# First norm's sum of squares from the token layout on ScalarE, early low parts on VectorE, and a fourth early feature tile

## The chip, the cores and the metric

The kernel runs on one core of one Trainium2 chip. The metric is the device time of one execution in microseconds (us). Three runs of the kernel before took 835.93, 838.29 and 835.86 us; the median is 835.93. A core has five engines, each with a queue of its own that it works through strictly in order: TensorE (PE in the trace; its weight loads are PEld), VectorE (DVE), ScalarE (ACT), GpSimdE (POOL) and SyncE (SP), which here only issues DMAs. Engines wait for each other through semaphores. SBUF is the on-chip working memory, and PSUM, which takes TensorE's results, has eight banks of 128 x 512 float32.

## The reference, cut to what matters

One decoder layer on 512 tokens of width 1024, all in float32. Only its beginning matters here:

```python
h = rms_norm(x, norm_mix_w)          # x * rsqrt(mean(x*x over the 1024 features) + 1e-6) * w
proj = h @ w_in                      # 1024 -> 5664 columns
z, xbc, dt_raw, q, k, v, f_raw = split(proj)
y_ssd = ssd_mixer(xbc, z, dt_raw)    # conv over 4 tokens, silu, chunked scan (4 chunks, 16 heads), gated norm
y_fox = fox_mixer(q, k, v, f_raw)    # attention with forgetting, 16 heads
x = x + concat(y_ssd, y_fox) @ w_out
x = x + conv_gated_mlp(rms_norm(x))  # 1024 -> 5632 -> 2816 -> 1024
```

## The kernel before, in words

Each float32 product is made of three multiplies on rounded halves: an operand is cast to a high part (ScalarE), and the low part is the operand less the high part (VectorE or GpSimdE). `mm3` (lines 108 to 112) issues high x high, low x high and high x low. `load_split` (lines 99 to 106) brings a 128 x 1024 weight tile in by SyncE (`wraw`, five buffers), casts it on ScalarE (`wh`, L104) and takes its low part (`wl`, L105). `wh` and `wl` have two buffers each, so a third weight tile can only be cast when TensorE has finished with the first.

The input comes twice: as `xT` (features on partitions, eight pieces `xr`), from which the operands `xh` (L181, ScalarE) and `xl` (L182, VectorE) are made, and as `x` (tokens on partitions, tile `x2`), which is the residual. The rms factor of the first norm is not applied to the input but to the results: `R` holds the factor of each token spread over 128 partitions, and `r` and `rhalf` hold it with tokens on partitions.

The work around the change, in the order of the program:

- Lines 192 to 214: eight warm-up multiplies into `spin`; then for each of the eight pieces the operands, the squares of the piece (L204 on ScalarE for pieces 1, 3, 5, 7, L206 on GpSimdE for the others), and on TensorE the dt/f projection `pdt` (L211, L212) and the first feature tile `b0` (weight `wxbc[8]`), 40 multiplies in all.
- Lines 232 to 239: the weight `second` (`wxbc[10]`), seven additions of the squares on VectorE (L234), four multiplies with a column of ones that sum over partitions into `spin` (L237), and `token_scale` (lines 136 to 144): mean and epsilon (L121), power -1/2 (L122, GpSimdE), a diagonal matrix (`diag`, L139), a multiply with ones that spreads it (`rbc`, L143), and the copy into `R` (L144, ScalarE).
- Line 597: three feature tiles are multiplied ahead of their turn (`early`): 8, 10 and 0. `feature_tile` (lines 222 to 230) issues 24 multiplies of 512 columns.
- `dt_f` (lines 262 to 316): a chain of small VectorE operations on `pdt` to the cumulative sums `cs` (L304, L307), which go out to DRAM (`cs_d`) and come back spread over partitions as `sc` (L395).
- `ssd_proj(g)` (lines 335 to 377): for six feature tiles the evacuation with `R` (`xp`, L344, VectorE), the convolution (L347 on ScalarE, three L351 on VectorE), tanh (L355) and its product (L356), and transposes (L360); then the two halves of `z` in `token_block` (four weight tiles), evacuated by L374 to L376.
- `ssd_scan(g)` (lines 385 to 450), four chunks: masked exponentials (L404, L409), their product with C B (L412), `yd` (L415), `yo` and the state.

Which engine takes a low part is told by the table `LOW_PART` (lines 36 to 51): the n-th call with a key takes the n-th letter, `d` for VectorE, `p` for GpSimdE; a key that isn't there means GpSimdE (`second`, and the four tiles of the first `z`). A scheduler orders the instructions of each engine by its own simulated timeline, with the code under `high_priority` first. So a change at the beginning also reorders rows that it doesn't touch. PSUM: three banks in pool `pg` (`pdt`, `b0` and `spin` to begin with), four in `pm` (`mbank`), one in `po`.

Of the kernel before, what the change touches and what calls it, by code (L numbers as in the profile page):

```python
# [8 lines left out]
F32 = mybir.dt.float32  # L9
F32R = mybir.dt.float32r  # L10
AF = mybir.ActivationFunctionType
ALU = mybir.AluOpType
# [3 lines left out]
P = 128  # L16
SEQ = 512
D = 1024
NK = D // P
NTB = SEQ // P  # L20
# [11 lines left out]

AHEAD = 2000
WARM = 8
ACT_SQ = (1, 3, 5, 7)
LOW_PART = {
    "feat": "pddddddddp",
    "o0": "dp",
# [17 lines left out]
def tile_hybrid_layer(  # L56
# [19 lines left out]
    nc = tc.nc  # L76
    act, dve, pool, pe = nc.scalar, nc.vector, nc.gpsimd, nc.tensor
# [5 lines left out]
    po = ctx.enter_context(tc.tile_pool(name="po", bufs=1, space=PSUM))  # L83
# [4 lines left out]
    def raw(ap):  # L88
        return ap.bitcast(F32)
# [3 lines left out]
    def low_part(key):  # L93
        order = LOW_PART.get(key, "p")
        n = taken.get(key, 0)
        taken[key] = n + 1
        return dve if order[n % len(order)] == "d" else pool

    def load_split(src, sub=None):
        r = wp.tile([P, 1024], F32, tag="wraw", name="wraw", bufs=5)  # L100
        nc.sync.dma_start(r, src)
        h = wp.tile([P, 1024], F32R, tag="wh", name="wh")
        l = wp.tile([P, 1024], F32R, tag="wl", name="wl")
        act.copy(h, r)  # L104
        (sub or dve).tensor_tensor(out=l, in0=r, in1=raw(h), op=ALU.subtract)  # L105
        return h, l

    def mm3(o, ah, al, bh, bl, start, stop, grouped=True):
        kw = {} if grouped else {"skip_group_check": True}
        pe.matmul(o, ah, bh, start=start, stop=False, **kw)  # L110
        pe.matmul(o, ah, bl, start=False, stop=False, **kw)  # L111
        pe.matmul(o, al, bh, start=False, stop=stop, **kw)  # L112

    def bank(name="g"):
        return pg.tile([P, 512], F32, tag="g", name=name)

    def mbank(name="m"):
        return pm.tile([P, 512], F32, tag="m", name=name)

    def rsqrt(dst, src, scale, shape):  # L120
        dve.tensor_scalar(out=dst, in0=src, scalar1=scale, scalar2=EPS, op0=ALU.mult, op1=ALU.add)  # L121
        pool.tensor_tensor(out=dst, in0=dst, in1=mhalf[:, 0 : shape], op=ALU.pow)  # L122
# [4 lines left out]
    ones = cp.tile([P, P], F32, tag="ones", name="ones")  # L127
# [6 lines left out]
    x2 = cp.tile([P, NTB, D], F32, tag="x2", name="x2")  # L134

    def token_scale(rr, bc, ss, diag_pool):
        rsqrt(rr, ss, 1.0 / D, NTB)
        dg = diag_pool.tile([P, NTB, P], F32, tag="diag", name="diag", bufs=1)
        dve.tensor_mul(  # L139
            dg, ident[:, None, :].broadcast_to([P, NTB, P]), rr[:, :, None].broadcast_to([P, NTB, P])  # L140
        )
        ps = mbank("rbc")
        pe.matmul(ps, ones, dg.rearrange("p a b -> p (a b)"), start=True, stop=True)  # L143
        act.copy(bc, ps)  # L144
# [6 lines left out]
    R = pa.tile([P, SEQ], F32, tag="R", name="R")  # L151
    r = cp.tile([P, NTB], F32, tag="r", name="r")
# [7 lines left out]
    px = px_ctx.enter_context(tc.tile_pool(name="px", bufs=1))  # L160
# [3 lines left out]
    def load_x(k):  # L164
        xr = px.tile([P, SEQ], F32, tag="xr", name="xr", bufs=NK)
        nc.sync.dma_start(xr, xT[k])
        return xr

    def load_first(half):
        c = slice(half * 512, (half + 1) * 512)  # L170
        w = px.tile([P, 512], F32, tag="wr", name="wr", bufs=2)
        nc.sync.dma_start(w, wxbc[8][:, c])
        return c, w

    def split_first(c, w):
        act.copy(first[0][:, c], w)
        dve.tensor_tensor(out=first[1][:, c], in0=w, in1=raw(first[0][:, c]), op=ALU.subtract)

    def split_x(k, xr):
        w = pc[:, C_MIX + k : C_MIX + k + 1]  # L180
        act.activation(xh[:, k, :], xr, AF.Copy, scale=w)  # L181
        dve.scalar_tensor_tensor(  # L182
            out=xl[:, k, :], in0=xr, scalar=w, in1=raw(xh[:, k, :]), op0=ALU.mult, op1=ALU.subtract
        )

    def load_dt():
        w = px.tile([P, NK, 32], F32, tag="wdr", name="wdr")
        nc.sync.dma_start(w.rearrange("p k m -> p (k m)"), wdtf)
        act.copy(wdt[:, :, 0:32], w)
        pool.tensor_tensor(out=wdt[:, :, 32:64], in0=w, in1=raw(wdt[:, :, 0:32]), op=ALU.subtract)  # L190

    pdt, b0, spin = bank(), bank(), bank()
    for _ in range(WARM):
        pe.matmul(spin[:, :P], ones, ones, start=True, stop=True)
    load_dt()
    sqs = []
    for k in range(NK):
        xr = load_x(k)
        if k == 0:
            nc.sync.dma_start(pc[:, 0:NK], pcol[:, 0:NK])  # L200
        split_x(k, xr)
        sq = px.tile([P, SEQ], F32, tag="sq", name="sq", bufs=NK)
        if k in ACT_SQ:
            act.activation(sq, xr, AF.Square)  # L204
        else:
            pool.tensor_tensor(out=sq, in0=xr, in1=xr, op=ALU.mult)  # L206
        sqs.append(sq)
        if k in (1, 3):
            split_first(*load_first(k // 2))
    for k in range(NK):  # L210
# [11 lines left out]
    def feature_tile(src, o=None):  # L222
        h, l = src if isinstance(src, tuple) else load_split(src, sub=low_part("feat"))
        o = bank() if o is None else o
        for k in range(NK):
            mm3(
                o, h[:, k * P : (k + 1) * P], l[:, k * P : (k + 1) * P], xh[:, k, :], xl[:, k, :],
                k == 0, k == NK - 1,
            )
        return o  # L230

    second = load_split(wxbc[10], sub=low_part("second"))
    for k in range(1, NK):
        dve.tensor_add(sqs[0], sqs[0], sqs[k])  # L234
    with tc.high_priority(AHEAD):
        for tb in range(NTB):
            pe.matmul(spin[:, tb : tb + 1], sqs[0][:, tb * P : (tb + 1) * P], ones[:, 0:1], start=True, stop=True)  # L237
        token_scale(r, R, spin[:, 0:NTB], px)
    dve.tensor_scalar(out=rhalf, in0=r, scalar1=0.5, scalar2=None, op0=ALU.mult)
    px_ctx.close()  # L240

# [352 lines left out]
    def urgent():  # L594
        return tc.high_priority(AHEAD)

    early = {8: b0, 10: feature_tile(second), 0: feature_tile(wxbc[0], po.tile([P, 512], F32, tag="o", name="j0"))}
    dt_f()
    st0 = ssd_proj(0)
    with urgent():  # L600
        m0 = ssd_scan(0, *st0)
    for tb in range(NTB):
        nc.sync.dma_start(x2[:, tb, :], x[tb * P : (tb + 1) * P, :])
    st1 = ssd_proj(1)
    for pair in range(2):
        out_proj((pair,), m0[2 * pair : 2 * pair + 2])
# [135 lines left out]
    def up_proj(fs, cuts):  # L742
        ws = [load_split(wup[f]) for f in fs]
        os = [bank("up") for _ in fs]
        w = SEQ // cuts
        for cut in range(cuts):
            s = slice(cut * w, (cut + 1) * w)
            for o, (h, l) in zip(os, ws):
                for k in range(NK):
                    ks = slice(k * P, (k + 1) * P)  # L750
                    mm3(
                        o[:, s], h[:, ks], l[:, ks], hh[:, k, s], hl[:, k, s], k == 0 and cut == 0, k == NK - 1,
                        grouped=cuts == 1,
                    )
        return os

    early = up_proj((0, NFF), 2)
# [9 lines left out]
    def gated(j):  # L767
        both = []
        for part in range(2):
            f = part * NFF + j  # L770
            o = early[part] if j == 0 else up_proj((f,), 1)[0]
            xp = pu.tile([P, SEQ], F32, tag="up", name="up", bufs=3)
            dve.tensor_mul(xp, o, R2)  # L773
            a = pu.tile([P, SEQ], F32, tag="ua", name="ua", bufs=5)
            cw = C_FCW + 3 * f
            act.activation(a, xp, AF.Identity, scale=pc[:, cw + 2 : cw + 3], bias=pc[:, C_FCB + f : C_FCB + f + 1])  # L776
            for s in range(1, 3):
                dve.scalar_tensor_tensor(  # L778
                    out=a[:, s:], in0=xp[:, : SEQ - s], scalar=pc[:, cw + 2 - s : cw + 3 - s], in1=a[:, s:],
                    op0=ALU.mult, op1=ALU.add,  # L780
                )
            both.append(a)
        act.activation(both[0], both[0], AF.Silu)
        return both
# [12 lines left out]
    for j in range(NH):  # L797
# [5 lines left out]
        k, val = gated(j + NH)  # L803
# [39 lines left out]
    for n, (quarter, _, tiles, start, adds) in enumerate(PRODUCTS):  # L843
# [7 lines left out]
        for u, (lo, hi) in enumerate(UNITS):  # L851
# [14 lines left out]
            for k, i, (lo_, _, h_, l_) in todo:  # L866
# [6 lines left out]
                if k == NH - 1:  # L873
                    for row, col, op, done in adds:
                        tb = row + i
# [85 lines left out]
```

## Time and profile before

| | |
|---|---|
| median of three runs | 835.93 us |
| the profiled execution's own time | 839.82 us |
| its span, first to last instruction | 838.0 us |
| mean granted TensorE clock over the span | 0.995 of full |
| busy: PE, DVE, ACT, POOL | 810.0, 630.9, 435.9, 290.5 us |
| idle TensorE before instructions of the first 140 us, as the trace names it | L212 1.44, L237 0.74, L360 0.75, L306 1.48, L428 0.50, L446 1.73, L415 0.34 us |
| chain that ended last | PE 73%, DVE 11%, issue 6%, POOL 3%, ACT 3%, DMA 2% |

Busy time is a modelled length from an instruction's start to its end; multiplies overlap, so the distance of two starts says more of TensorE's pace than a length. "Idle before" an instruction names what ended the wait of its engine. The times are those of one execution; the profiled one took 3.89 us more than the median of the runs.

### The profile page before, as it was taken

How to read it: one execution, taken by the hardware profiler on the slowest of the kernel's cores; microseconds unless marked ns; L12 is line 12 of the kernel's file. 1: busy time of each engine (PE TensorE's matmuls, PEld its weight loads, DVE VectorE, ACT ScalarE, POOL GpSimd, SP SyncE). 2: the span in 40 equal slices, each digit the busy share in tenths (PEclk: the TensorE clock that was granted, in tenths of full speed). 3: DMA queues.
4: the chain of work that ended last, by engine and by line, in shares of the span. 5: the costliest groups of instructions: out<-in, count | busy, mean ns of one | idle time of the engine just before them, and what ended most of it. 6: DMA issues, size and time to landing. Idle time of an engine off the chain costs nothing.

```text
span 838.0 us, 12428 instructions
## 1 busy us (share of the span) xinstructions
PE 810.0 (97%) x4590; PEld 700.4 (84%) x4590; DVE 630.9 (75%) x1015; ACT 435.9 (52%) x845; POOL 290.5 (35%) x281
## 2 busy tenths in 40 slices
PE   8999989899979999899999999999999999999997
PEld 5788879779979899799898898888888888888885
DVE  7596898775759798898999667666666666887744
ACT  5346645434456687576566255444433444656531
POOL 4125253365535445125233423333333332133120
PEclk9999999999989999999999999999999999999999
DMA  8424332341333333243422244233233223399992
GB/s 315 158 83 131 101 94 85 104 136 51 113 102 106 100 100 112 84 120 101 126 72 66 90 121 134 100 98 101 101 101 99 82 96 101 115 253 182 208 190 84
DMA packets 31565, 98.76 MB, mean 118 GB/s; under 512 B 4048, under 2 KB 5136, under 8 KB 31504
## 3 DMA queue, kind: packets, MB, share of 16 engines
q1 hardware_dynamic: 28048, 86.43, 31.9%
q0 software_dynamic: 3456, 11.54, 7.6%
q8 instruction: 36, 0.59, 0.3%
q14 instruction: 25, 0.20, 0.1%
HBM read 91.56 MB, written 2.20 MB: 112 GB/s over the span
## 4 chain that ended last, share of the span: by engine, by line
PE 73%; DVE 11%; issue 6%; POOL 3%; ACT 3%; DMA 2%; SPq 0%; DVEq 0%; POOLq 0%; ACTq 0%
PE up L112 10%; PE up L111 9%; PE up L110 9%; PE pq L111 4%; PE pq L112 4%; PE pq L110 4%; PE po L112 3%; PE po L111 3%; PE po L110 3%; DVE xs L351 2%; PE Y L110 2%; PE Y L112 2%; PE Y L111 2%; PE o L580 2%; PE pT L566 1%
## 5 line engine op out<-in xcount | busy, mean ns | idle before, releaser
L104 ACT CAST wh<-wraw 128x1024 fp32r<-128x1024 f32 x103 | 108.5, 1053 | 137.6 <-PE up L111 72.1
L110 PE MATMUL pq<-wh,xh 128*128 128x256 f32 x512 | 146.7, 289 | 0.0
L112 PE MATMUL pq<-wh,xl 128*128 128x256 f32 x512 | 146.7, 287 | 0.0
L111 PE MATMUL pq<-wl,xh 128*128 128x256 f32 x512 | 145.6, 285 | 0.5 <-DVE wl L105 0.5
L112 PE MATMUL up<-hh,wl 128*128 128x512 f32 (+1 forms) x368 | 140.2, 381 | 0.2 <-DVE wl L105 0.2
L111 PE MATMUL up<-hl,wh 128*128 128x512 f32 (+1 forms) x368 | 139.9, 380 | 0.0
L110 PE MATMUL up<-hh,wh 128*128 128x512 f32 (+1 forms) x368 | 139.8, 380 | 0.0
L105 POOL TENSOR_TENSOR wl<-wraw,wh 128x1024 fp32r<-128x1024 f32 x31 | 75.1, 2424 | 108.9 <-ACT wh L104 99.9
L105 DVE TENSOR_TENSOR wl<-wraw,wh 128x1024 fp32r<-128x1024 f32 x72 | 89.5, 1243 | 20.0 <-ACT wh L104 19.9
L111 PEld LDWEIGHTS pq<-wl,xh 128*128 128x128 f32 x512 | 98.2, 192 | 1.9 <-DVE wl L105 0.9
L110 PEld LDWEIGHTS pq<-wh,xh 128*128 128x128 f32 x512 | 98.0, 192 | 1.9 <-issue 1.2
L112 PEld LDWEIGHTS pq<-wh,xl 128*128 128x128 f32 x512 | 98.2, 192 | 0.7 <-issue 0.5
L112 PEld LDWEIGHTS up<-hh,wl 128*128 128x128 f32 x368 | 69.2, 188 | 13.5 <-DVE wl L105 0.4
L110 PEld LDWEIGHTS up<-hh,wh 128*128 128x128 f32 x368 | 69.1, 188 | 13.3 <-issue 0.2
L111 PEld LDWEIGHTS up<-hl,wh 128*128 128x128 f32 x368 | 69.2, 188 | 13.2
L773 DVE TENSOR_TENSOR up<-up,R 128x512 f32<-128x512 f32 x44 | 30.3, 691 | 57.0 <-PE up L112 57.0
L778 DVE SCALAR_TENSOR_TENSOR ua<-up,pc,ua 128x511 f32<-128x511 f32 (+1 forms) x88 | 67.2, 766 | 3.2 <-ACT ua L776 1.7
L526 POOL TENSOR_SCALAR bias<-cum,tokS 128x256 f32<-128x256 f32 (+1 forms) x32 | 22.5, 711 | 91.2 <-DVE nm L541 91.2
L545 ACT ACTIVATE prob<-prob,nm 128x128 f32<-128x128 f32 (+1 forms) x64 | 35.9, 562 | 29.6 <-DVE nm L541 29.3
L254 DVE TENSOR_TENSOR x<-po,x 128x512 f32<-128x512 f32 x64 | 43.3, 684 | 10.1 <-PE po L112 9.5
L734 ACT CAST wh<-T 128x1024 fp32r<-128x1024 f32 (+1 forms) x30 | 29.3, 978 | 37.5 <-PE Z L112 15.6
L735 DVE TENSOR_TENSOR wl<-T,wh 128x1024 fp32r<-128x1024 f32 (+1 forms) x30 | 33.8, 1133 | 19.7 <-ACT wh L734 19.7
(237 smaller groups left out, 1862.9 us busy)
## 6 DMA issues: line engine op xcount, KB each, us to landing
wraw<-in_wup_dram SPq DMA_DIRECT2D x44, 512.0 KB, 3.3
wraw<-in_wqkv_dram SPq DMA_DIRECT2D x24, 512.0 KB, 3.3
T<-in_wdown_dram POOLq DMA_DIRECT2D x20, 512.0 KB, 7.8
wraw<-in_wout_dram SPq DMA_DIRECT2D x16, 512.0 KB, 3.3
wraw<-in_wxbc_dram SPq DMA_DIRECT2D x11, 512.0 KB, 4.6
T<-in_wdown_dram SPq DMA_DIRECT2D x10, 512.0 KB, 5.1
wraw<-in_wdown_dram SPq DMA_DIRECT2D x10, 512.0 KB, 3.7
wraw<-in_wz_dram SPq DMA_DIRECT2D x8, 512.0 KB, 3.3
```

The lines of the kernel that those rows point to most:

```text
L104: act.copy(h, r)
L105: (sub or dve).tensor_tensor(out=l, in0=r, in1=raw(h), op=ALU.subtract)
L110: pe.matmul(o, ah, bh, start=start, stop=False, **kw)
L111: pe.matmul(o, ah, bl, start=False, stop=False, **kw)
L112: pe.matmul(o, al, bh, start=False, stop=stop, **kw)
L254: dve.tensor_add(dst, o, dst)
L526: (dve if qb == 2 else pool).tensor_scalar(out=b, in0=cum[:, :n], scalar1=-1.0, scalar2=edge, op0=ALU.mult, op1=ALU.add)
L545: act.activation(p, p, AF.Exp, scale=-1.0, bias=nm[:, qb : qb + 1], accum_out=sm[:, qb : qb + 1])
L734: act.copy(h[:, :n], src[:, :n])
L735: dve.tensor_tensor(out=l[:, :n], in0=src[:, :n], in1=raw(h[:, :n]), op=ALU.subtract)
L773: dve.tensor_mul(xp, o, R2)
L778: dve.scalar_tensor_tensor(out=a[:, s:], in0=xp[:, : SEQ - s], scalar=pc[:, cw + 2 - s : cw + 3 - s], in1=a[:, s:], op0=ALU.mult, op1=ALU.add,
```

## The change

The squares are no longer made from the `xT` pieces and added up. The four loads of `x2` move to the front of the program, ScalarE squares each token block with an accumulated sum per token, and `token_scale` reads that sum. The low parts of `second` and of tile 0's weight are put on VectorE, and tile 0's weight is loaded ahead with `second`. A fourth tile, 1, is multiplied early, into a bank of `pm`. Since tile 0's weight no longer takes a letter of the key `feat`, the letters move on by one tile. In all, the low parts of wxbc[10], wxbc[0] and wxbc[7] go from GpSimdE to VectorE, and that of wxbc[1] from VectorE to GpSimdE.

```diff
-ACT_SQ = (1, 3, 5, 7)
...
         split_x(k, xr)
-        sq = px.tile([P, SEQ], F32, tag="sq", name="sq", bufs=NK)
-        if k in ACT_SQ:
-            act.activation(sq, xr, AF.Square)
-        else:
-            pool.tensor_tensor(out=sq, in0=xr, in1=xr, op=ALU.mult)
-        sqs.append(sq)
...
-    second = load_split(wxbc[10], sub=low_part("second"))
-    for k in range(1, NK):
-        dve.tensor_add(sqs[0], sqs[0], sqs[k])
+    second, third = [load_split(wxbc[j], sub=dve) for j in (10, 0)]
+    for tb in range(NTB):
+        nc.sync.dma_start(x2[:, tb, :], x[tb * P : (tb + 1) * P, :])
     with tc.high_priority(AHEAD):
+        ssx = px.tile([P, NTB], F32, tag="ssx", name="ssx")
         for tb in range(NTB):
-            pe.matmul(spin[:, tb : tb + 1], sqs[0][:, tb * P : (tb + 1) * P], ones[:, 0:1], start=True, stop=True)
-        token_scale(r, R, spin[:, 0:NTB], px)
+            sq = px.tile([P, D], F32, tag="sq", name="sq", bufs=2)
+            act.activation(sq, x2[:, tb, :], AF.Square, accum_out=ssx[:, tb : tb + 1])
+        token_scale(r, R, ssx, px)
...
-    early = {8: b0, 10: feature_tile(second), 0: feature_tile(wxbc[0], po.tile([P, 512], F32, tag="o", name="j0"))}
+    early = {8: b0, 10: feature_tile(second), 0: feature_tile(third, po.tile([P, 512], F32, tag="o", name="j0"))}
+    early[1] = feature_tile(wxbc[1], mbank("j1"))
...
-    for tb in range(NTB):
-        nc.sync.dma_start(x2[:, tb, :], x[tb * P : (tb + 1) * P, :])
```

Line numbers of the changed kernel are smaller by one up to the squares, by eight for the second `pc` load, and by six from line 239 on (L104 becomes L103, L355 becomes L349). On ScalarE, the first weight casts stood in this order, in the kernel before (`sq` are the squares of pieces, `mv` a small exponential):

```order
L181 ACTIVATE xh<-xr,pc 128x512 x2
L204 ACTIVATE sq<-xr 128x512
L104 CAST wh<-wraw 128x1024
L271 ACTIVATE mv<-v 128x1
L104 CAST wh<-wraw 128x1024 x2
L144 COPY R<-rbc 128x512
```

and stand so in the changed kernel (`sq,ssx` are the squares of token blocks and their sums):

```order
L180 ACTIVATE xh<-xr,pc 128x512 x4
L103 CAST wh<-wraw 128x1024 x2
L231 ACTIVATE sq,ssx<-x_86 128x1024 x4
L103 CAST wh<-wraw 128x1024
L265 ACTIVATE mv<-v 128x1
L103 CAST wh<-wraw 128x1024
L143 COPY R<-rbc 128x512
```

The four squares stand behind the casts of wxbc[10] and wxbc[0], and the copy into `R` behind four casts instead of three, the last that of wxbc[2].

On TensorE, `rbc` stood after the second tile and seven multiplies of tile 0 (two of tile 0's stood ahead of the second tile); in the changed kernel it stands behind the whole of both tiles, 48 multiplies (`j_271` is tile 0's bank, `j_296` tile 1's):

```order
L109 MATMUL j_271<-xh,wh 128x512
L110 MATMUL j_271<-xl,wh 128x512
L111 MATMUL j_271<-xh,wl 128x512
L142 MATMUL rbc<-diag,ones 128x512
L109 MATMUL j_296<-xh,wh 128x512
L110 MATMUL j_296<-xl,wh 128x512
```

Of SyncE's queue, the loads of `x2` stand right behind the weights wxbc[10] and wxbc[0], ahead of wxbc[1], of two small tiles (`v`, `dsk`), and of wxbc[2] and wxbc[3]; before, they stood behind all of these.

Where `cs` is about to be ready, ScalarE had these rows in the kernel before (`gz` and `th` evacuate the first half of `z`; the cast is that of the fourth `z` weight; `xp<-xs` is the tanh of feature tile 3):

```order
L355 ACTIVATE xp<-xs 128x512
L365 COPY x_tok<-xT 128x128 x4
L374 ACTIVATE gz<-pq,rhalf 128x256
L375 ACTIVATE th<-pq,rhalf 128x256
L374 ACTIVATE gz<-pq,rhalf 128x256
L375 ACTIVATE th<-pq,rhalf 128x256
L104 CAST wh<-wraw 128x1024
```

and in the changed kernel:

```order
L359 COPY x_tok<-xT 128x128 x4
L368 ACTIVATE gz<-pq,rhalf 128x256
L369 ACTIVATE th<-pq,rhalf 128x256
L368 ACTIVATE gz<-pq,rhalf 128x256
L369 ACTIVATE th<-pq,rhalf 128x256
L103 CAST wh<-wraw 128x1024
L349 ACTIVATE xp<-xs 128x512
```

The tanh of tile 3 now stands behind the cast of the fourth `z` weight. On VectorE, the product after that tanh (L356) stands ahead of L307 in both kernels, and two of the products of `gz` (L376) have moved from behind `cs` (L304) to ahead of it.

## Rows read from the trace of the kernel before

**Rows 1.** Stage windows: from:to, length, busy PE, PEld, DVE, ACT, POOL, clock, DMA share, GB/s.

```profile
13.10:23.30 10.20, 7.78 (x36) 4.82 (x34) 9.16 (x15) 2.85 (x5) 3.44 (x2) 1.00 0.92 366
...
32.60:67.50 34.90, 32.68 (x198) 28.92 (x196) 34.31 (x59) 17.53 (x35) 7.59 (x3) 1.00 0.28 90
67.50:85.60 18.10, 18.09 (x130) 17.14 (x131) 9.25 (x17) 13.40 (x42) 9.53 (x7) 1.00 0.46 142
85.60:130.00 44.40, 41.84 (x225) 34.67 (x224) 42.35 (x52) 23.30 (x51) 17.43 (x12) 1.00 0.31 98
...
247.00:838.00 591.00, 579.90 (x3184) 500.95 (x3182) 445.92 (x729) 313.64 (x564) 189.08 (x196) 1.00 0.41 115
```

**Rows 2.** Timeline of TensorE: start, length, instruction, [idle before <-what ended it].

```profile
12.24 0.63 PE L212 MATMUL g<-xl,wdt 128*32 128x512 f32 x1
12.66 0.63 PE L111 MATMUL g<-xl,wh 128*128 128x512 f32 x1
...
18.14 0.42 PE L212 MATMUL g<-xl,wdt 128*32 128x512 f32 x1 [1.44 <-DVE xl L182]
...
20.98 0.39 PE L111 MATMUL g<-xl,wh 128*128 128x512 f32 x1
21.21 0.40 PE L112 MATMUL g<-xh,wl 128*128 128x512 f32 x1
...
23.27 0.47 PE L110 MATMUL j<-xh,wh 128*128 128x512 f32 x1
...
85.56 1.89 PE L415 MATMUL yd<-xdt,sc 128*128 128x64 f32 x16
```

**Rows 3.** Timeline of VectorE and of GpSimdE at the same moment.

```profile
14.57 3.52 DVE L182 SCALAR_TENSOR_TENSOR xl<-xr,pc,xh 128x512 fp32r<-128x512 f32 x2
...
14.86 2.67 POOL L105 TENSOR_TENSOR wl<-wraw,wh 128x1024 fp32r<-128x1024 f32 x1 [2.63 <-ACT wh L104]
```

**Rows 4.** Timeline of ScalarE: the cast of tile 0's weight.

```profile
21.41 1.04 ACT L104 CAST wh<-wraw 128x1024 fp32r<-128x1024 f32 x1 [6.50 <-PE g L111]
```

**Rows 5.** Squares of token blocks with accumulated sum, in the second norm: min/median/max ns.

```profile
L760 ACT ACTIVATE junk<-x x4: 1045/1050/1065, 489.1 to 492.3; 128x1024 f32<-128x1024 f32 x4
```

**Rows 6.** Loads of x2: issues with first and last start, and their time to landing.

```profile
L603 SPq DMA_DIRECT2D x<-in_x_dram x4: 328/423/697, 12.0 to 14.9; - x4
...
DMA to landing us min/median/max: 9.7/9.7/10.6
```

**Rows 7.** Timeline of VectorE from R to the first scan product.

```profile
32.58 1.29 DVE L344 TENSOR_TENSOR xp<-g,R 128x512 f32<-128x512 f32 x2 [0.94 <-ACT R L144]
...
38.39 1.23 DVE L105 TENSOR_TENSOR wl<-wraw,wh 128x1024 fp32r<-128x1024 f32 x1
...
47.41 2.38 DVE L285 TENSOR_SCALAR u<-u,v,sb 128x128 f32<-128x128 f32 x1
...
67.04 0.41 DVE L304 TENSOR_TENSOR_SCAN cs<-ones,ad 128x128 f32<-128x128 f32 x1
67.38 0.73 DVE L376 SCALAR_TENSOR_TENSOR gz<-th,gz 128x256 f32<-128x256 f32 x2
...
68.63 0.28 DVE L307 TENSOR_SCALAR cs<-cs,pt 128x128 f32<-128x128 f32 x1
...
80.24 1.22 DVE L412 TENSOR_TENSOR sc<-sc,cb 128x1024 f32<-128x1024 f32 x1 [1.56 <-ACT sc L409]
```

**Rows 8.** Timeline of GpSimdE: first and fourth low part of the first z.

```profile
47.30 2.39 POOL L105 TENSOR_TENSOR wl<-wraw,wh 128x1024 fp32r<-128x1024 f32 x1 [21.38 <-ACT wh L104]
...
70.99 2.40 POOL L105 TENSOR_TENSOR wl<-wraw,wh 128x1024 fp32r<-128x1024 f32 x1 [5.27 <-ACT wh L104]
```

**Rows 9.** The chain that ended last: start, length, what.

```profile
87.48 4.73 DMA sc<-cs_d
```

**Rows 10.** Timeline of TensorE: the instruction after its longest wait.

```profile
240.12 0.45 PE L539 MATMUL S<-ks,qs 128*128 128x128 f32 x1 [4.53 <-DMA ks<-ks]
```

**Rows 11.** Stage window around that wait, columns as in rows 1.

```profile
238.50:245.30 6.80, 5.18 (x21) 5.02 (x22) 3.11 (x12) 3.01 (x10) 1.54 (x4) 0.51 0.18 67
```

More of the change, by code (lines that the diff above doesn't have):

```diff
@@ L195, in tile_hybrid_layer @@
     load_dt()
-    sqs = []
     for k in range(NK):
```

## The prediction

> **What bounds the kernel now.** I read the stage windows first [rows 1], then the timelines of the engines at the seams between them, then the chain of waits. Over most of the span TensorE is the bound: from 247 us on it is busy 579.90 of 591 us. In the part that the change reorders, the bound changes hands. From 13.1 to 23.3 us TensorE is busy 7.78 of 10.20: it waits for VectorE, once for 1.44 us [rows 2], where two operands that should take 0.7 each last 3.52 together, with a GpSimdE low part of 2.67 beside them [rows 3]. From 32.6 to 67.5 VectorE is busy 34.31 of 34.90. From 67.5 to 85.6 TensorE has no gap (18.09 of 18.10) and VectorE is half idle. From 85.6 to 130 VectorE is the bound again (42.35 of 44.40). So time that the change saves on TensorE at the start is not yet time saved: it has to pass two stages that VectorE paces.
>
> **The change part by part.**
>
> *Start of TensorE.* Removed: seven additions of squares and one held-up operand on VectorE, four squares on ScalarE, four on GpSimdE, the low parts of wxbc[10] and wxbc[0] on GpSimdE, the four sums into `spin`. TensorE's first 40 multiplies then have their operands in time and run at its own pace. That pace is 0.42 us per multiply up to 13.1 us and 0.23 after it (12.24 to 12.66, 20.98 to 21.21; the lengths fall from 0.63 to 0.39) [rows 2]. Fourteen of the 40 have started by 12.66, counted in that timeline. I take 16 at 13.1, since the low part of the first weight comes some 0.8 us earlier without an addition before it; the other 24 take 24 x 0.23 = 5.5, so the second tile starts at 18.6 and not at 23.27: 4.7 earlier. With 14 or 18 at 13.1 it is 4.2 or 5.2. If the faster pace came a microsecond later, another 0.5 would be lost.
>
> *Squares on ScalarE, a new wait.* The cast of wxbc[0] needs the buffer of the first tile's weight, as it does before (6.50 us idle, released by TensorE) [rows 4]; now the four squares, the cast of wxbc[1] and everything later on ScalarE are queued behind it. The cast runs from 18.5 to 19.6. A square with its sum took 1.05, four starts 489.1 to 492.3, so 1.07 apiece [rows 5]: done at 23.9. Mean 0.2, power 1.0, `diag` 0.7: 25.8. `rbc` needs it behind 48 multiplies, at 18.6 + 48 x 0.23 = 29.6. The cover is 3.8 us; beyond it each microsecond costs one.
>
> *Loads.* Before, the loads of `x2` are issued from 12.0 to 14.9 and land 9.7 to 10.6 later, 21.7 to 25.5 [rows 6]. They pass three weights of 0.524 MB, at 366 GB/s [rows 1] 1.43 us each, so the last lands at 25.5 - 4.3 = 21.2; its square would start at 22.8. Cover 1.6. The passed weights land up to 4 x 1.43 = 5.7 later: wxbc[1] some 23 to 24, where its cast can start at 24.1, and TensorE needs it at 30.5. I cost this at nothing.
>
> *R.* `rbc` ends where the buffer for wxbc[2] comes free, and that cast stands ahead of the copy into `R`, its low part ahead of the first evacuation. 29.6 + 1.05 (cast) + 1.2 (low part) = 31.85, against 32.58 [rows 7]. Of 4.7 us on TensorE, VectorE gets 0.7. The fourth early tile keeps TensorE fed meanwhile.
>
> *VectorE to `cs`.* One low part fewer (1.23, next instruction 1.15 later or so) and two products of `gz` more (0.73 for both) [rows 7]: -0.4. A GpSimdE low part holds VectorE up: at 47.41 a small operation beside it lasts 2.38 [rows 7], until the low part of 47.30 ends [rows 8]. Three of z's four low parts fall into this stretch before, and I count three again. With 0.7 from R, `cs` comes 0.5 to 1.1 earlier, at 66.
>
> *The fourth low part.* Before, it starts at 70.99 [rows 8], after L307 (68.63). Now its cast stands ahead of the tanh for which L356, and behind it L307, wait. Cast to 67.2, low part 67.3 to 69.7, L356 held until then, L307 at 70.3: 1.7 later than before. If VectorE is not held there, L307 comes at 68.0, 0.6 earlier. I take 70.3, since the row at 47.41 shows the hold-up.
> The Trainium skill, page "SBUF — State Buffer", section "SBUF: two separate sides", says that the two engines share a port pair as an exclusive lock for a whole instruction, and that a VectorE operation with two SBUF inputs is among those shut out. L356 has two, so by the rule L307 is at 70.3; a VectorE read from PSUM would pass. The trace agrees in the one place above, with 2.38 us.
>
> *Scan.* From L307 to the product L412 it was 11.6 us (68.63 to 80.24) [rows 7]: 81.9, ending 83.1. `yd` starts there, against 85.56 [rows 2], where TensorE was still busy with a feature tile. TensorE itself would be ready at 85.56 - 4.7 + about 1.4 for its new wait on L356, 82.3. So `yd` is 2.5 earlier, and with it the load of `sc` for the third chunk (4.73 us) [rows 9], which opens VectorE's next full stage.
>
> *85 to 130 us.* VectorE has one low part more (wxbc[7], +1.2) and is spared one GpSimdE low part (-2.2 by the hold-up above): 1.0 less. The lead becomes 3.5, say 3.4. Behind this the order of rows is the same to the end, so the lead is kept.
>
> Sum, against the profiled execution of 839.82 us: 839.82 - 3.4 = 836.4. The median of the runs stands 3.89 below that execution, so I predict 835.93 - 3.4 = 832.5 us. Bounds: nothing gained after R, 0.7; all of TensorE's 4.7 carried on and the 1.0, 5.7.
>
> **The rivals.**
>
> *VectorE takes all but its own lead.* If the stage from 85 us follows `cs` and not `yd`, only 0.7 + 0.4 remain: 834.8. For it: VectorE has 0.59 us of slack before 67.5 [rows 1]. Against: between 67.5 and 85.6 it waited for TensorE and ScalarE.
>
> *The clock.* TensorE, 4 us ahead, must wait for the transposes of feature tile 2. Ahead of them the new order has 120 full multiplies (x 0.23 = 27.6), 89 half-wide ones at half of that (10.2) and some 2.2 for `rbc` and three transposes, so it is there at 58.6 to 59; the product L356 for them comes about 4 us ahead of `cs` by the timeline, at 62. A wait of about 3 us is new in this stage. Before, a wait of 4.53 us [rows 10] was followed by a granted clock of 0.51 (2.4 to 1.2 GHz) between 238.5 and 245.3 [rows 11]; waits up to 1.73 were not. If the clock falls, 6.8 us at half pace put `yd` to 84.8, a lead of 0.8, and 1.8 in the end: 834.1.
> The Trainium skill, "TensorE: Matmul & The Clock Gate", section "HAM oscillation — how this bites in real kernels", has this rule against the change: a TensorE that runs dry between bursts begins the next one cold. The trace shows it once, as told.
>
> *Not held.* If L307 is at 68.0, `yd` follows TensorE at 81.3: 4.3, and 1.0: 830.6.
>
> *Slower.* The slack of the scan is the mechanism: L412 ended at 81.4 and `yd` came at 85.56, so L307 may come 4.1 later before `yd` does. If three instructions ahead of it are held for 2.2 to 2.4 each, L307 is at 75.5 to 76.3, `yd` is 3.5 later, and after the 1.0 the time is 838.4. For it: four GpSimdE low parts now crowd into the stretch before L307 and a late one of wxbc[1] is new. Against: three of them were there already.
>
> **How the numbers follow.** Forecast 0.48, own range 831.0 to 834.0; VectorE takes all 0.17; clock 0.13; not held 0.14; slower 0.08. About 0.3%, 2.5 us, is what a measurement of this kernel can tell from no change: faster means below 833.4. That is four fifths of the forecast (0.38), the case not held (0.14) and a little of the two middle ones (0.04): 0.56. Slower is the last rival, 0.08; the rest, 0.36, is within. Leaving out the slower case and the outer half of the one not held, the range is 830.3 to 836.2.
>
> **What would show it.** Right: the second feature tile starts near 18.6, first `xp` near 31.9, L307 near 70 with a 2.4 us instruction before it, `yd` near 83, TensorE's wait around 60 us without a fall of the clock. Wrong: squares that end after 29 us; a first `xp` later than 32.6; `yd` later than 85.6; a granted clock near 0.5 between 60 and 70; or a lead at 130 us that is not there at 165.

## The result, and the profile after

The changed kernel took 830.76 (the profiled execution, span 829.0), 829.64 and 829.33 us; a fourth run, 883.88 us at a mean granted clock of 0.851, was a disturbed one, which the comparison leaves out and the median of all four, 830.2, includes. The ratio to the kernel before is 0.9915, interval 0.9890 to 0.9941. A second set of runs, from 829.02 to 831.65, gave 0.9924 (0.9910 to 0.9938): 6.4 us of 837.3. The prediction was 832.5, a gain of 3.4. The direction was right and the gain is about twice the forecast. The kernel before is itself slower than its first three runs said: in the later sets, of 11 to 18 runs each, its median was 837.06 to 837.58, not 835.93.

In the profiles below, lines behind L239 of the kernel before are 6 lower (L415 is now L409), L105 is L104, and L110 to L112 are L109 to L111; an experiment's own can be one higher again.

TensorE after, timeline: start, length, instruction, [idle before <- what ended it].

```profile
10.69 0.53 PE L203 MATMUL g<-xh,wdt 128*64 128x512 f32 x1
11.06 0.40 PE L109 MATMUL g<-xh,wh 128*128 128x512 f32 x1
11.30 0.39 PE L204 MATMUL g<-xl,wdt 128*32 128x512 f32 x1
...
17.52 0.39 PE L111 MATMUL g<-xh,wl 128*128 128x512 f32 x1
17.75 0.39 PE L109 MATMUL g<-xh,wh 128*128 128x512 f32 x1
...
55.57 0.66 PE L354 MATMUL xT<-ident,xs 128*128 128x128 f32 x4 [1.63 <-ACT x_tok L359]
...
61.40 0.63 PE L354 MATMUL xT<-ident,xs 128*128 128x128 f32 x4 [1.58 <-DVE xs L350]
...
81.61 2.00 PE L409 MATMUL yd<-xdt,sc 128*128 128x64 f32 x16 [0.25 <-DVE sc L406]
...
94.02 0.60 PE L440 MATMUL yT<-ident,y 128*128 128x128 f32 x4
...
118.75 0.66 PE L440 MATMUL yT<-ident,y 128*128 128x128 f32 x4 [1.44 <-DVE y L435]
...
125.06 0.55 PE L354 MATMUL xT<-ident,xs 128*128 128x128 f32 x3 [1.64 <-ACT x_tok L359]
...
139.97 0.60 PE L440 MATMUL yT<-ident,y 128*128 128x128 f32 x4
...
216.28 0.60 PE L440 MATMUL yT<-ident,y 128*128 128x128 f32 x4
...
231.91 0.30 PE L533 MATMUL S<-ks,qs 128*128 128x128 f32 x1 [1.70 <-DMA ks<-ks]
```

The same engine before, at places that [rows 2] don't show.

```profile
99.39 0.60 PE L446 MATMUL yT<-ident,y 128*128 128x128 f32 x4
...
123.99 0.66 PE L446 MATMUL yT<-ident,y 128*128 128x128 f32 x4 [1.73 <-DVE y L441]
...
142.71 0.62 PE L446 MATMUL yT<-ident,y 128*128 128x128 f32 x4
...
158.64 0.50 PE L110 MATMUL po<-wh,msh 128*128 128x512 f32 x1 [1.33 <-ACT th L375]
163.84 0.50 PE L110 MATMUL po<-wh,msh 128*128 128x512 f32 x1 [1.45 <-ACT msh L448]
...
221.66 0.60 PE L446 MATMUL yT<-ident,y 128*128 128x128 f32 x4
```

Read as leads of one kernel over the other: 5.5 us at the first multiply behind the opening 40 (17.75 against 23.27 [rows 2]), `yd` 3.95 (81.61 against 85.56), first `yT` 5.37, second 5.24, third 2.74, eighth 5.38, the first S 8.21 (231.91 against 240.12 [rows 10]), the end 9.0 by the spans.

A lead is time won only where the same work lies ahead of both places. Counted in the timelines, that holds for `yd`, for the eighth `yT` and for S, but for the small sums into `spin` that the change removes. It doesn't hold for the first `yT`: between `yd` and it TensorE has 49 multiplies of feature tiles before and 42 after, and the other seven, 1.6 us, come behind it. Behind the eighth `yT` nothing is left of the code that the change touches, and from S on the order of rows is the same on every engine. So the last 3.6 us between these two executions need their own cause; 2.8 of them are there at S, whose wait for `ks` was 4.53 us and is 1.70.

ScalarE, VectorE and GpSimdE after.

```profile
17.72 1.05 ACT L103 CAST wh<-wraw 128x1024 fp32r<-128x1024 f32 x1 [3.12 <-PE g L110]
18.68 1.06 ACT L231 ACTIVATE sq<-x 128x1024 f32<-128x1024 f32 x1
...
22.76 0.18 ACT L231 ACTIVATION_READ_ACCUMULATOR sq<-x 128x1 f32 x1
```

```profile
24.31 2.92 DVE L138 TENSOR_TENSOR diag<-ident,r 128x512 f32<-128x512 f32 x1 [1.10 <-POOL r L121]
...
30.82 1.28 DVE L338 TENSOR_TENSOR xp<-g,R 128x512 f32<-128x512 f32 x2
...
65.30 0.42 DVE L298 TENSOR_TENSOR_SCAN cs<-ones,ad 128x128 f32<-128x128 f32 x1
...
66.98 2.47 DVE L350 SCALAR_TENSOR_TENSOR xs<-xp,xs 128x512 f32<-128x512 f32 x1 [0.60 <-ACT xp L349]
69.37 0.28 DVE L301 TENSOR_SCALAR cs<-cs,pt 128x128 f32<-128x128 f32 x1
...
80.33 1.22 DVE L406 TENSOR_TENSOR sc<-sc,cb 128x1024 f32<-128x1024 f32 x1 [1.19 <-ACT sc L403]
```

```profile
24.29 2.39 POOL L104 TENSOR_TENSOR wl<-wraw,wh 128x1024 fp32r<-128x1024 f32 x1
...
66.50 2.40 POOL L104 TENSOR_TENSOR wl<-wraw,wh 128x1024 fp32r<-128x1024 f32 x1 [7.24 <-ACT wh L103]
```

The hold-up that the prediction put ahead of `cs` is there: L350 lasts 2.47 us beside the fourth low part. It came a second time, unforeseen, on `diag`, 2.92 us beside the low part of wxbc[1].

One more of the kind, from the kernel before: a GpSimdE low part, and two taps of the convolution on VectorE beside it, 3.63 us for both. The changed kernel has no such low part there.

```profile
106.86 2.66 POOL L105 TENSOR_TENSOR wl<-wraw,wh 128x1024 fp32r<-128x1024 f32 x1 [5.49 <-ACT wh L104]
107.23 3.63 DVE L351 SCALAR_TENSOR_TENSOR xs<-xp,half_w,xs 128x510 f32<-128x510 f32 x2
```

Windows after: from:to, length, busy PE, PEld, DVE, ACT, POOL, granted clock, DMA share, GB/s.

```profile
7.60:11.00 3.40, 3.40 (x8) 2.46 (x9) 2.94 (x5) 3.04 (x5) 0.00 (x0) 0.50 1.05 394
...
30.80:66.00 35.20, 31.99 (x208) 28.95 (x207) 34.53 (x62) 18.70 (x41) 8.57 (x3) 1.00 0.23 75
66.00:81.60 15.60, 15.16 (x104) 13.65 (x103) 8.84 (x15) 8.53 (x27) 9.69 (x7) 1.00 0.46 142
...
126.00:230.00 104.00, 104.00 (x728) 94.25 (x726) 75.61 (x117) 50.96 (x120) 51.69 (x43) 0.98 0.33 107
127.10:130.50 3.40, 3.40 (x12) 2.26 (x12) 3.33 (x7) 1.40 (x5) 0.00 (x0) 0.51 0.79 278
...
232.80:236.30 3.50, 3.50 (x16) 3.31 (x16) 2.80 (x10) 2.97 (x10) 1.21 (x2) 0.51 0.39 136
```

The clock (0.5 is 1.2 of 2.4 GHz) is low from 7.6 to 11.0, from 127.1 to 130.5, behind waits of 1.44 and 1.64, and from 232.8 to 236.3, behind the wait of 1.70 for `ks`; near 60 it isn't. From 126 to 230 TensorE has no gap.

### The profile page after: what moved, and what is told of

It reads as the page before. It is cut to its first block, busy times and chain, and to the rows that moved or that the text cites. A ratio compares the mean times of both kernels' runs of the same rounds, so it can differ in the third digit from the quotient of the medians.

```text
span 829.0 us, 12398 instructions
## 1 busy us (share of the span) xinstructions
PE 806.8 (97%) x4582; PEld 699.4 (84%) x4582; DVE 625.4 (75%) x1010; ACT 439.5 (53%) x849; POOL 282.3 (34%) x275
## 4 chain that ended last, share of the span: by engine, by line
PE 75%; DVE 11%; issue 6%; POOL 3%; DMA 3%; ACT 2%; SPq 0%; DVEq 0%; POOLq 0%; ACTq 0%
PE up L111 10%; PE up L109 10%; PE up L110 10%; PE pq L109 4%; PE pq L111 4%; PE pq L110 4%; PE po L109 4%; PE po L111 3%; PE po L110 3%; PE Y L109 2%; PE Y L111 2%; PE Y L110 2%; DVE xs L345 2%; PE o L574 2%; POOL ms L121 1%
## 5 line engine op out<-in xcount | busy, mean ns | idle before, releaser
L103 ACT CAST wh<-wraw 128x1024 fp32r<-128x1024 f32 x103 | 108.4, 1052 | 137.0 <-PE up L110 72.1
L111 PE MATMUL pq<-wh,xl 128*128 128x256 f32 x512 | 147.3, 288 | 0.0
L110 PE MATMUL pq<-wl,xh 128*128 128x256 f32 x512 | 146.3, 286 | 0.5 <-DVE wl L104 0.5
L109 PE MATMUL pq<-wh,xh 128*128 128x256 f32 x512 | 146.1, 288 | 0.0
L111 PE MATMUL up<-hh,wl 128*128 128x512 f32 (+1 forms) x368 | 140.2, 381 | 0.2 <-DVE wl L104 0.2
L110 PE MATMUL up<-hl,wh 128*128 128x512 f32 (+1 forms) x368 | 139.9, 380 | 0.0
L109 PE MATMUL up<-hh,wh 128*128 128x512 f32 (+1 forms) x368 | 139.8, 380 | 0.0
L104 DVE TENSOR_TENSOR wl<-wraw,wh 128x1024 fp32r<-128x1024 f32 x74 | 91.9, 1243 | 19.8 <-ACT wh L103 19.8
L109 PEld LDWEIGHTS pq<-wh,xh 128*128 128x128 f32 x512 | 98.4, 193 | 2.3 <-issue 1.6
L110 PEld LDWEIGHTS pq<-wl,xh 128*128 128x128 f32 x512 | 98.5, 192 | 1.7 <-DVE wl L104 0.7
L111 PEld LDWEIGHTS pq<-wh,xl 128*128 128x128 f32 x512 | 98.5, 192 | 1.2 <-issue 1.0
L104 POOL TENSOR_TENSOR wl<-wraw,wh 128x1024 fp32r<-128x1024 f32 x29 | 71.1, 2450 | 79.5 <-ACT wh L103 70.6
L111 PEld LDWEIGHTS up<-hh,wl 128*128 128x128 f32 x368 | 69.2, 188 | 13.8 <-DVE wl L104 0.4
L109 PEld LDWEIGHTS up<-hh,wh 128*128 128x128 f32 x368 | 69.1, 188 | 13.2 <-issue 0.2
L110 PEld LDWEIGHTS up<-hl,wh 128*128 128x128 f32 x368 | 69.2, 188 | 13.0
```

## Experiments

**The two kernels once more.** No edit.

> The kernel before, unchanged, once more. It leaves nothing out. Theory (the change is worth what it has won by 230 us, 5.4 us; what comes on top in the two profiled executions, 2.8 us less waiting for ks ahead of the first S and 0.9 us of clock behind it, is a matter of the single execution): ratio 1.000 within 0.002; the last milestones before the wait (yT for the eighth time, 221.7) within 0.3 us of the first profile, while the wait of S for ks is another one than 4.53, anywhere from 1 to 5. Rival (the long wait belongs to the order of the kernel before): 4.5 within 0.3 again, and a half clock of 6.8 us behind it.

> The changed kernel, unchanged, once more. Theory: ratio 0.992 to 0.994 (5.4 us plus or minus the ks wait); the wait of S for ks anywhere from 1 to 5 us. The granted clock rises to full between 11 and 13.4 us at the start; if it is 13.4 and not 11.0, the second feature tile starts near 18.6 and not at 17.7, as predicted. Rival (the opening belongs to the change): ks wait 1.7 again, second tile at 17.7 again, ratio 0.990.

Measured: 837.06 us, ratio 1.0000 (0.9988 to 1.0012); and 830.46, ratio 0.9924. TensorE before, then after, in the second profiles:

```profile
221.87 0.60 PE L446 MATMUL yT<-ident,y 128*128 128x128 f32 x4
...
238.46 0.30 PE L539 MATMUL S<-ks,qs 128*128 128x128 f32 x1 [2.66 <-DMA ks<-ks]
```

```profile
215.78 0.60 PE L440 MATMUL yT<-ident,y 128*128 128x128 f32 x4
...
231.47 0.30 PE L533 MATMUL S<-ks,qs 128*128 128x128 f32 x1 [1.76 <-DMA ks<-ks]
```

The eighth `yT` is where it was, within 0.2 and 0.5 us. The wait of S before is 2.66 and not 4.53, so it isn't the same in two executions of one kernel. The lead ahead of that wait is 6.1 us this time, 5.4 the first; at S it is 7.0, and at the end 6.9. The changed kernel's wait, though, is 1.76 again, as the rival had it.

**The parts of the change.** Squares alone (the low parts of both weights on GpSimdE, wxbc[0] loaded at its turn as before, three early tiles); only the lines that differ from the changed kernel:

```
- second, third = [load_split(wxbc[j], sub=dve) for j in (10, 0)]
+ second = load_split(wxbc[10], sub=low_part("second"))
  ...
- early = {..., 0: feature_tile(third, ...)}
- early[1] = feature_tile(wxbc[1], mbank("j1"))
+ early = {..., 0: feature_tile(wxbc[0], ...)}
```

> Only the squares are changed (ScalarE from the token layout, with the early loads of it): the low parts of wxbc[10] and wxbc[0] are on GpSimdE as before and three feature tiles are early, not four. Theory (the gain is TensorE's start, and that comes from taking the squares off VectorE and GpSimdE): TensorE's first tile still ends at 17.7 to 18.6, since both low parts have time; at least 4 of the 5.4 us: 830.5 to 832.5 beside a before of 836.5, ratio 0.993 to 0.995. Rival (the parts share the gain about equally): 2 us, ratio 0.9975 or more.

The changed kernel without the fourth early tile (the line `early[1] = ...` alone is taken out):

> The changed kernel with three early feature tiles and not four. Theory: TensorE, ahead by 5.5 us, runs out of banks near 29.5 and waits until the first xp, about 2 us; of these it loses in the changed kernel 1.6 twice in any case, between 55 and 62, so the whole is slower than the changed kernel by 0 to 1 us: 830 to 831.5, ratio 0.992 to 0.994. Rival (the fourth tile carries the lead): slower than the changed kernel by 2 us or more, ratio 0.9945 or more.

The changed kernel with both low parts on GpSimdE (`sub=pool` for `sub=dve`):

> The changed kernel with the low parts of wxbc[10] and wxbc[0] on GpSimdE and not on VectorE; ScalarE, SyncE and the rest of the order are the same, and TensorE has only one early tile taken in another order with its neighbour. Theory (between 14 and 24 us neither engine has much to do, both low parts are in time): first xp within 0.3 us of 30.6 to 30.8, yd within 0.3 of 81.4 to 81.6, ratio 0.991 to 0.9935, as the changed kernel. Rival (this part of the change carries a third of the gain, as the step of 1.8 us from squares alone to three early tiles suggests): 1.5 to 2 us slower than the changed kernel, ratio 0.994 to 0.9955.

Measured: 834.0, ratio 0.9968 (0.9953 to 0.9983); 832.2, 0.9949 (0.9933 to 0.9965); 831.43, 0.9927 (0.9900 to 0.9954). By the ratios the squares alone bring 2.7 us, the early split of wxbc[0] and the low parts on VectorE some 1.6 more, the fourth tile some 2.1, with intervals that overlap from step to step. Neither theory on the squares had it (4 or more, or 2 or less), and the fourth tile is worth more than I expected, about what its rival said. What the engine of the low parts is worth stays open: the interval of that kernel holds the ratio of the changed one and most of the rival's range too. Its profile, of a run slower than its median, has the first `xp` at 32.27 and not within 0.3 of 30.8. TensorE with the squares alone, and with three tiles:

```profile
73.49 0.50 PE L109 MATMUL g<-xh,wh 128*128 128x512 f32 x1 [2.87 <-ACT wh L103]
...
219.07 0.60 PE L440 MATMUL yT<-ident,y 128*128 128x128 f32 x4
```

```profile
30.44 0.50 PE L109 MATMUL g<-xh,wh 128*128 128x512 f32 x1 [1.90 <-DVE xp L338]
...
216.89 0.60 PE L440 MATMUL yT<-ident,y 128*128 128x128 f32 x4
```

In each a part left out comes back as a wait of TensorE: 2.87 us for a cast, and behind it a clock of 0.50 from 74.1 to 80.9; 1.90 for the first `xp`, since no bank is free. Both eighth `yT` stand behind 14 multiplies of half width more than in the changed kernel, 1.7 us, so they can't be set against its 216.28 as they are. The profile with three tiles is the fastest of its six runs (829.66) and has its S at 232.00, as late as the changed kernel; the price of the fourth tile stands on the times of the runs alone.

**R early.** The squares ahead of wxbc[0]:

```
- second, third = [load_split(wxbc[j], sub=dve) for j in (10, 0)]
+ second = load_split(wxbc[10], sub=dve)
  ...
  token_scale(r, R, ssx, px)
+ third = load_split(wxbc[0], sub=dve)
```

> The changed kernel with the weight wxbc[0] loaded and split behind the squares, not ahead of them; four early tiles and low parts on VectorE as in the changed kernel. ScalarE then starts the squares when x2 lands (14.4 in the kernel with the squares alone) and not when TensorE has ended its first tile (17.7), and rbc stands behind one early tile and not behind two. Theory (TensorE's idle time and its clock set the lead, R does not): R comes 5 us earlier, first xp near 25.5 and not 30.8, and yd near 78 to 80, but the multiplies ahead of the ks wait are the same, so at most the two waits of 1.6 us near 55 to 62 go: ratio 0.989 to 0.993. Rival (R was what the kernel after waited for, as VectorE is full from 32 to 66): 4 us or more faster than the changed kernel, ratio 0.987 or less.

Measured: 829.97, ratio 0.9915 (0.9889 to 0.9942), no different from the changed kernel within some 2 us. VectorE and TensorE:

```profile
26.37 1.29 DVE L339 TENSOR_TENSOR xp<-g,R 128x512 f32<-128x512 f32 x2 [0.83 <-ACT R L143]
```

```profile
72.60 0.39 PE L110 MATMUL pq<-wl,xh 128*128 128x256 f32 x1 [2.46 <-POOL wl L104]
76.63 1.55 PE L410 MATMUL yd<-xdt,sc 128*128 128x64 f32 x12
...
214.75 0.60 PE L441 MATMUL yT<-ident,y 128*128 128x128 f32 x4
```

R and `yd` are 4.5 and 5.0 us earlier than in the first profile after, the eighth `yT` 1.5. But 24 full and 15 half-wide multiplies, some 7.3 us, that stood ahead of `yd` now come behind it, so `yd` is earlier in the order and not by a gain of TensorE. At S, with the same work ahead, this profile leads by 2.6 us; it is the fastest of six runs, 826.8, 3.2 below their median. The lead on VectorE's path is not a lead of the kernel that the times show.

**The hold-up ahead of `cs`.** The fourth low part of z on VectorE:

```
+ "z0": "pppd",
```

> The changed kernel with the fourth low part of z on VectorE and not on GpSimdE, so that L350 ahead of cs isn't held for 2.47 us but has 1.22 ahead of it. Theory (at yd TensorE and VectorE are level, TensorE waits 0.25 there): nothing or up to 0.3 us, ratio 0.992 to 0.993 as the changed kernel. Rival (the hold-up keeps yd back, as the prediction had it): 1.2 to 1.7 us faster than the changed kernel, ratio 0.990 to 0.991.

Measured: 825.75, ratio 0.9869 (0.9846 to 0.9891): 4.7 us faster than the changed kernel. Both theories missed that. VectorE and TensorE:

```profile
67.09 0.29 DVE L302 TENSOR_SCALAR cs<-cs,pt 128x128 f32<-128x128 f32 x1
```

```profile
85.54 1.67 PE L410 MATMUL yd<-xdt,sc 128*128 128x64 f32 x14
...
227.63 0.60 PE L441 MATMUL yT<-ident,y 128*128 128x128 f32 x4
...
234.93 0.22 PE L534 MATMUL S<-ks,qs 128*128 128x128 f32 x1
```

Without the hold-up `cs` is 2.3 us earlier (67.09 against 69.37), but the edit also moved the order of other work: 24 full multiplies more, 5.5 us, stand ahead of `yd`, 70 half-wide ones ahead of the eighth `yT` and 16 ahead of S. So it confirms the hold-up and doesn't price it. In the profile the gain lies behind S: S is 3.0 us later than in the changed kernel, with no wait ahead of it, and from S to the end it takes 588.6 us and not 597.1.

**The clock at the start.** `WARM = 14` for 8.

> The changed kernel with 14 instead of 8 multiplies of ones ahead of the work; they fill TensorE from 1 to 7.2 us, and the first real multiplies, which start at 5.17, are 2 us later, ahead of a wait of 0.97. Theory (the first tile's length is a matter of the granted clock, which in the changed kernel fell from 7.6 to 11.0): without a fall the first tile ends 1.2 us earlier, near 16.5, and the time is 1 us better or, if R is late, the same: ratio 0.990 to 0.9925. Rival (the clock falls all the same, or the late start of the real multiplies is not made up): slower by 0.5 to 2 us, ratio 0.993 to 0.995.

Measured: 832.06, ratio 0.9939 (0.9919 to 0.9960): slower by 1.6 us, as the rival said, though the intervals overlap, and not by its mechanism. The clock was full from 4.3 to 120.4 us, the first `xp` came at 29.51, 1.3 us earlier, the eighth `yT` at 215.29, 1.0 earlier. Then S waited 3.31 us for `ks` and started at 232.53: the gain was lost there.

**The copy of ks.** Its first pair issued by ScalarE's queue, in the changed kernel and in the kernel before:

```
- nc.sync.dma_start(raw(ks[hd][other, :, :]), ...)
+ (nc.scalar if pair == 0 else nc.sync).dma_start(raw(ks[hd][other, :, :]), ...)
```

> The changed kernel with the two copies of ks of the first pair issued by ScalarE's queue and not by SyncE's, where they stand behind a weight of 0.524 MB. Theory (the first S waits for the landing of ks, 5.5 us in the changed kernel and 8.3 in the kernel before, because the copy shares its queue with that weight): landing near 3 us, the wait of 1.7 ahead of the first S gone, no half clock behind it: 1.5 to 2.9 us faster than the changed kernel, ratio 0.989 to 0.9905. Rival (the copy is slow by itself, or by the transfers of other queues): landing 5 us or more, the same ratio as the changed kernel, 0.992 to 0.993.

> The kernel before with the two copies of ks of the first pair issued by ScalarE; the order behind the first S is moved by this in the same way as in the changed kernel. Theory (the gain of the change is made ahead of the eighth yT, 5.4 to 6.1 us, and has nothing to do with what comes behind S): 7 to 8 us faster than the kernel before, 829 to 830, ratio 0.9905 to 0.9920; the distance to the changed kernel with the same edit (822.6) is 6 to 7 us. Rival (part of the gain lies in the wait for ks or behind it, which this edit changes for both): the distance is 4 us or less, or 9 or more.

Measured: 822.64, ratio 0.9823 (0.9798 to 0.9847); and 831.31, ratio 0.9924 (0.9907 to 0.9941). The first is 7.8 us faster than the changed kernel, yet not for the reason given:

```profile
231.68 0.30 PE L533 MATMUL S<-ks,qs 128*128 128x128 f32 x1 [1.61 <-DMA ks<-ks]
```

The wait is still 1.61, the copy lands after 5.4 us. What went is behind S. Windows of the changed kernel, second profile, and of the kernel with the edit:

```profile
250.00:345.00 95.00, 89.99 (x694) 85.38 (x693) 81.62 (x177) 63.90 (x152) 42.27 (x46) 1.00 0.32 97
```

```profile
250.00:345.00 95.00, 94.97 (x727) 90.60 (x727) 80.85 (x196) 68.06 (x160) 44.97 (x53) 1.00 0.33 103
```

Five us of idle TensorE are gone, in a stretch where the edit also moved the order of work; and the clock, which fell for 3.4 us behind S in the changed kernel, stayed full there. The distance between the two edited kernels is 1.0% or 8.4 us, between the bounds that I had set, and its interval, some 5 to 12 us, reaches both theories. In their profiles, which lie 10.3 us apart, 5.67 of it is there at the eighth `yT`, 2.9 more at S. S in the kernel before with the edit, and, from 238.17 to 240.2, the queue that holds nothing but the copies (packets, MB, share of 16 engines):

```profile
240.29 0.45 PE L539 MATMUL S<-ks,qs 128*128 128x128 f32 x1 [4.55 <-DMA ks<-ks]
```

```profile
q10 hardware_dynamic: 9, 0.03, 4.8%
```

In the trace's list of packets one of the instruction queue, 16384 B, runs from 236.59 to 238.18. By 237.98 all packets of the copies but the last few have ended; these start as that one ends, run one after another until 240.12, and S starts. In the changed kernel with the edit the same packet runs from 229.87 to 231.30, and S starts at 231.68, 0.4 us behind it and not 2.1. This reads as one DMA engine whose share of the copy stood behind a load of code. It isn't the whole account: with the squares alone the first copy took 7.12 us and landed at 234.50, before the code packet of that profile ended, at 234.92. No run moved that load alone. Whether the order of the kernel before makes the wait long (4.53, 2.66, 4.55) and that of the changed one short (1.70, 1.76, 1.61), or chance, stays open.

**Together.** The squares ahead of wxbc[0] with the edit on `ks`, and then also the fourth low part of z on VectorE:

> The kernel with the squares ahead of wxbc[0], and the copies of ks of the first pair issued by ScalarE. Theory: both gains add up: 1.0 us from the squares (eighth yT at 214.75 and not at 215.8 to 216.3), 7.8 from the order behind S: 821.5 to 822, ratio 0.980 to 0.982. Rival: the lead of 1 us is lost in the wait for ks, 822.6, as without the squares moved.

> The same with the fourth low part of z on VectorE as well. Theory: what this edit gave alone (4.7 us) was the order behind S, which the edit on ks gives already; so nothing more: 820.5 to 823, ratio 0.979 to 0.983. Rival (it gave the freed VectorE ahead of cs): 2 us or more faster, 820 or less.

Measured: 824.7, ratio 0.9834 (0.9817 to 0.9851), where the gains don't add up; and 820.78, 0.9803 (0.9783 to 0.9822), as its theory said, the fastest here, 16.5 us under the kernel before, though not told apart from 0.9823.

## Why the prediction was right in kind and half in size

The sum had 2.5 us at `yd`, 1.0 up to 130 us and nothing behind it. The first pair of profiles shows 3.95 at `yd`, some 0.8 in the second step, and more behind it.

- **TensorE's start: right in kind, the largest term mis-sized, by 0.9.** "I take 16 at 13.1" failed: 20 had started, because the faster pace came at 11.0 (10.69 to 11.06, then 0.24) and not at 13.1. The opening 40 end at 17.75 and not 18.6. The pace of 0.42 up to 13.1 was read in one execution of the kernel before and taken for the changed one. In three profiles with the start of the kernel before, the half clock lasts 6.8 us or more; with that of the changed kernel it lasts 3.4 in three and doesn't come in a fourth (that of `"z0": "pppd"`, where the 40 end at 16.6). So its shorter stay may belong to the change, but no run varied it alone.
- **Squares: right.** They end at 22.9 (23.9), and `rbc`, at 28.64, did not wait. The cover was thinner than I had it, 1.4 and not 3.8 us, as `diag` was held and ended at 27.2. Their loads cost nothing.
- **R and `cs`: right, 1.0 and 0.7 earlier.** First `xp` 30.82 for 31.85, the start's 0.9 carried on; `cs` at 65.30 for 66. The 0.4 that the stage between them was to lose didn't come: 34.48 us against 34.46 [rows 7].
- **The hold-up: right.** L301 at 69.37 for 70.3, the same 0.9. By the rule of the Trainium skill, page "SBUF — State Buffer", section "SBUF: two separate sides", a VectorE operation with two SBUF inputs is shut out for the whole of a GpSimdE instruction that reads SBUF and started first; the trace agrees, with 2.47 us on L350 and 2.92 on `diag`.
- **Scan: right, 0.6 too long.** From L301 to `yd` it took 12.24 us, not 12.8. `yd` is at 81.61 for 83.1: the 0.9 and the 0.6 together.
- **85 to 130 us: right.** The GpSimdE low part of 106.86 and its hold-up are gone, and VectorE has one low part more, at 108.96. From `yd` to the second `yT` TensorE idled 2.22 us before and 1.43 after, in the second profiles 2.93 and 1.42: 0.8 and 1.5 for the forecast 1.0.
- **"Behind this the order of rows is the same to the end, so the lead is kept": the step that failed.** From the second to the eighth `yT` the lead was lost and won back. The half clock at 127 and the wait of 1.64 ahead of it bring it down to 2.74 at the third `yT`; then two waits of the kernel before, 1.33 and 1.45, are gone. It came out level (5.24 and 5.38) in the first pair by luck; in the second it fell from 6.84 to 6.09. And the wait for `ks` isn't a constant that both kernels share: between the profiles it gave 2.8, 0.9 and 2.9 us more at S. I had read it in one execution, [rows 10], and carried it over. Of the 3.0 us that the second set of runs has beyond the forecast, the mis-sized start and scan give some 1.5 by the first pair of profiles; the rest lies behind `yd`, most of it in this step, and what makes the wait for `ks` long or short stays open.
- **The rivals.** TensorE's new wait near 60 came as two, of 1.63 and 1.58, and the clock stayed full there, as forecast. (The price of that rival was too low: half pace for 6.8 us on a TensorE that is ready at 82.3 gives 85.7, not 84.8.) VectorE did not take all but its own lead: `yd` led by 3.95, not 1.1. The slower case needed L307 at 75.5; it was at 69.37.
- **The baseline.** From 1.1 to 1.7 us of the forecast time was luck: I subtracted from the 835.93 of three runs, and the later sets gave 837.1 to 837.6. Against those the forecast would have been 834 and the miss larger.

## What to carry to other kernels

Sum up the waits of the engine that is full at the end (here TensorE) up to a place with the same work ahead of it, rather than follow the lead of the one that paces a stage. Ahead of the eighth `yT` TensorE idles 12.4 and 12.5 us before, 9.6 and 9.3 after: about half of the lead of 5.4 and 6.1; R 4.5 us earlier brought nothing that the times show. Before a milestone is compared, count what stands ahead of it in both orders: seven multiplies moved behind the first `yT`, or 24 behind `yd`, look like a gain of 1.6 or 5.5 us. Don't carry a lead past a wait that a DMA ends until a second profile has shown that wait; and once an order is made by a scheduler, a small edit anywhere moves waits far behind it by more than its own price.

## What was not expected of the hardware

- The clock at the start differs between executions of one kernel: low to 13.1 in the first profile before (by the pace of 0.42), from 8.0 to 11.4 and again from 18.2 to 21.6 in the second; from 7.6 to 11.0 and from 7.4 to 10.8 in the two after. With 14 multiplies of ones ahead it didn't fall there at all.
- Waits of much the same length ahead of S were followed by a fall of the clock or not: of 1.70 and 1.76 us in the changed kernel they were, of 1.61 (with the edit on `ks`), 2.32 (squares ahead of wxbc[0]) and 2.86 (three tiles) they weren't.
- What a low clock cost can be read off the stretch from S to the end, with the same order of rows each time, only roughly: 595.7 and 595.8 us without one behind S (squares ahead of wxbc[0], three early tiles), 596.9 to 597.5 with one of 3.4 us in five profiles, 597.9 with one of 6.8 (first before), but 598.4 with one of 3.4 where the low parts were on GpSimdE.
- Each square with a sum is followed on ScalarE by an instruction of its own, 0.18 to 0.19 us, that reads the sum.
- A code load is one packet that took 1.4 to 1.6 us of a DMA engine's time in the two profiles read for it, and the last packets of a copy ran in the 2 us behind it in one of them.
